# Layer-1 retention: transposes for identity matmuls, gate tiles moved around the scores, modulation steps paused

## The chip, the cores and the metric

One core of one Trainium2 chip runs the whole program. The engines are TensorE (PE: matmuls, with its weight loads shown as PEld), VectorE (DVE), ScalarE (ACT), GpSimd (POOL) and SyncE (SP, which here issues DMAs). The metric is device time in microseconds, the median of several runs. The profile is of one execution, with its own time.

## The reference, cut to what matters

The program is a two-layer backbone over 256 latent and 256 context tokens of width 1024. Each layer normalises and modulates the tokens, mixes them, adds the result, and then does the same with a SwiGLU feed-forward network (FFN). Layer 0 mixes by windowed attention and a gated linear recurrence, layer 1 by retention with 4 heads. The shift, scale and gate vectors of the modulation come from a product of the condition vectors with a 1024 x 6144 matrix for each layer.

For each retention head the reference computes, from the normalised streams h (1024 wide):

```
q, k (256 wide), v, g (512 wide)  = h @ w_in         # q and g for latent tokens only
q, k                              = rope(q), rope(k)  # latent tokens
o   = (decay * (q k^T)) v                             # both directions; keys: latent and context
y   = rms_norm(o) * silu(g)
out = concat over heads (y) @ w_out
```

## The kernel before, in words

Tokens lie along the free dimension, features on the 128 partitions. Every matmul operand is split into a high and a low part in float32r (hi = the rounded copy, lo = the rest), and a product is three matmuls: hi x hi, hi x lo, lo x hi (`mm3`, lines 333 to 338). Weights come as blocks of 128x128, 8 blocks to a piece: one DMA of 512 KB, a copy on ACT (line 268) and a subtraction on DVE (line 269). `take` hands out blocks in the order of the calls and splits two pieces ahead (`LOOK`); four split pieces exist at a time, so a fifth waits until the first has been used. A column tile of 128 outputs over the 8 blocks of the streams is one piece and 24 matmuls of 256 columns.

The text of the program is not the order of execution. A planner (the scheduler of the tile framework) sorts the instructions of each engine at compile time: the earlier an instruction is called, the higher its rank, but an instruction of lower rank goes first if the planner reckons that the engine would otherwise be idle. On the chip each engine then runs its list in order. So a wait appears where the planner's reckoning of another engine was too fast.

Small work is spread between the matmuls by ticks. `mm3` counts columns, and each 1600 columns call `tick`, which makes one step of each lane that is open and counts towards a modulation step: when the count reaches `modt`, one step is called and `modt` is taken off the count. A count goes on growing while `modt` is 10 ** 9. A modulation step loads 512 KB and makes one or two products of 128x1024 on DVE (line 233).

The retention runs head by head (lines 1171 to 1180). For each head: `ret_kq` makes K and Q, applies rope on DVE (`rope`, lines 1033 to 1039) and splits them; `ret_gate` makes two column tiles of the gate and applies Silu on ACT; `ret_scores` makes K^T Q, 24 matmuls from line 1106, multiplies by the decay matrix on DVE (line 1109) and splits; a second `ret_gate` makes the other two gate tiles; `ret_values` sums the token-major streams by the scores (`sums`) and projects the sums by the value weights (`project`); `ret_norm` (lane r) normalises and gates.

The token-major streams `htok` are made once, in head 0, by `tok_lane` (lane t, lines 1045 to 1057): for each of 4 token blocks and each half of the features, 4 pairs of matmuls against a float32r identity (`identr`) transpose hi and lo and add them in PSUM, and a split follows. `start` runs the lane's first step within `ret_kq(0)`, ahead of the rope; `drain` calls what is left of it before the values.

In head 0, K and Q come from `first_group`, which multiplies while the norm of the tokens is still being computed and corrects the result on DVE (`fix`); its four pieces are held until the context part of K is done.

Of the kernel before, what the change touches and what calls it, by code (L numbers as in the profile page):

```python
# [7 lines left out]
F32 = mybir.dt.float32  # L8
BF16 = mybir.dt.bfloat16
F32R = mybir.dt.float32r  # L10
I32 = mybir.dt.int32
AF = mybir.ActivationFunctionType
ALU = mybir.AluOpType
# [3 lines left out]
P = 128  # L17
D = 1024
KD = 8
L = 256  # L20
NT = 512
LAT = slice(0, 256)
# [10 lines left out]
N_PIECE = N_BLOCKS // PIECE  # L33
LOOK = 2
LN = 2
MODT = [4.6, 5.5, 4, 4]
QD = 3
FA = 2
PES = [3]
# [29 lines left out]
def hybrid_kernel(ctx, tc, xT, wst, mw0, mwT, small, cbc, cst, imask, dmat, out, order):  # L69
    nc = tc.nc  # L70
    V, A, T, G = nc.vector, nc.scalar, nc.tensor, nc.gpsimd

    cp = ctx.enter_context(tc.tile_pool(name="cp", bufs=1))
# [11 lines left out]
    def nm(s):  # L85
        uid[0] += 1
        return f"{s}_{uid[0]}"

    def u(shape=(P, NT), dt=F32):
        return up.tile(list(shape), dt, tag="u", name=nm("u"))  # L90
# [4 lines left out]
    def mmb():  # L95
        return pm.tile([P, NT], F32, tag="mm", name=nm("mm"))
# [37 lines left out]
    ident = con[:, C_ID:C_ID + P]  # L134
# [108 lines left out]
    modt = [MODE]  # L243
# [56 lines left out]
    def push(lane, gen):  # L300
        lanes.setdefault(lane, []).append(gen)
# [19 lines left out]
    def drain(lane):  # L321
        q = lanes.get(lane, [])
        while q:
            for _ in q.pop(0):
                pass
# [14 lines left out]
    def cut(a, s):  # L340
        return (a[0][:, s], a[1][:, s])
# [3 lines left out]
    def group(src, cols, ks, act, sls=(ALL,), kouter=True, banks=None):  # L345
        ps = banks or [mmb() for _ in cols]
        n = len(ks)
        ws = {}

        def one(i, j, sl):  # L350
            if (i, j) not in ws:
                ws[i, j] = take(src, ks[i], cols[j])
            mm3(ps[j][:, sl], ws[i, j], cut(act[i], sl), i == 0, i == n - 1)

        if len(sls) > 1 and not kouter:
            for j in range(len(cols)):
                for i in range(n):
                    one(i, j, sls[0])
            for sl in sls[1:]:
                for j in range(len(cols)):  # L360
                    for i in range(n):
                        one(i, j, sl)
            return ps
        for p, sl in enumerate(sls):
            if p:
                drain('c')
            if kouter and p == 0:
                for i in range(n):
                    for j in range(len(cols)):
                        one(i, j, sl)  # L370
            else:
                for j in range(len(cols)):
                    for i in range(n):
                        one(i, j, sl)
        return ps
# [151 lines left out]
    HS = [(a[:], b[:]) for a, b in h]  # L527

    K8 = list(range(8))
# [72 lines left out]
    def start(lane, gen):  # L602
        next(gen)
        push(lane, gen)
# [300 lines left out]
    tokgroup('ein', E_I, HS, itok_done)  # L905
    modt[0] = MODT[0]

    for hd in range(4):
        c = E_H + 3 * hd
        pg = group('ein', [c, c + 1, c + 2], K8, HS, kouter=False)  # L910
# [7 lines left out]
    for hd in range(4):  # L918
        pg = group('ein', [E_G + hd], K8, HS, kouter=False)
# [57 lines left out]
    def ffn(l, hs, streams, nxt, nl):  # L977
# [3 lines left out]
        for half in range(2):  # L981
            us = []
            jt = 0
            while jt < 11:
# [26 lines left out]
                jt += n  # L1011
                modt[0] = MODT[1 + 2 * l]
            if half == 1:
# [12 lines left out]
    ffn(0, hs, (0, 1), n1, nl)  # L1026
    HS = [(a[:], b[:]) for a, b in hh]

    modt[0] = MODT[2]
    O_K, O_Q, O_V, O_G = 0, 2, 4, 8  # L1030
    y1 = [None] * 16

# [5 lines left out]
            V.tensor_tensor(t[:, 1], d, rsin, ALU.mult)  # L1038
            V.tensor_tensor(o, t[:, 0], t[:, 1], op)

    identr = cp.tile([P, P], F32R, tag="idr", name="idr")
    A.activation(identr[:], ident, AF.Copy)
    htok = [[None, None] for _ in range(4)]

    def tok_lane():

        for st in range(4):
            for half in range(2):
                ps = axb((P, 4, P))
                for i in range(4):  # L1050
                    hi, lo = cut(HS[half * 4 + i], slice(st * P, (st + 1) * P))
                    T.matmul(ps[:, i, :], hi, identr[:], start=True, stop=False)
                    T.matmul(ps[:, i, :], lo, identr[:], start=False, stop=True)
                th, tl = u((P, 4, P), F32R), u((P, 4, P), F32R)
                split(ps[:], th[:], tl[:])
                htok[st][half] = (th, tl)
                yield
# [27 lines left out]
        split(qf[:], qhi[:], qlo[:])  # L1085
        return kk, (qhi, qlo)

    def ret_gate(hd, d2):
        c = 12 * hd + O_G + 2 * d2
        pg = group('oin', [c, c + 1], K8, HS, sls=(LAT,), kouter=False)  # L1090
        g = u((P, 2, L))
        for i in range(2):
            A.activation(g[:, i, :], pg[i][:, LAT], AF.Silu)
        return g

    def ret_scores(hd, kk, qq):
        dm = [u((P, 2, L)), u((P, 2, L))]
# [17 lines left out]
    def ret_values(hd, pp):  # L1115

        o = [mmb(), mmb()]
        gs = []

        def sums(k):  # L1120
            ps = axb()[:, 0:L]
            for st in range(4):
                mm3(ps, [t[:, k % 4, :] for t in htok[st][k // 4]], pp[st], st == 0, st == 3)
            t = u((P, 2, L), F32R)
            split(ps, t[:, 0], t[:, 1])
            gs.append((t[:, 0], t[:, 1]))

        def project(k):
            for dv in range(4):
                w = take('oin', k, 12 * hd + O_V + dv)  # L1130
                mm3(o[dv // 2][:, (dv % 2) * L:(dv % 2 + 1) * L], w, gs[k], k == 0 and dv % 2 == 0, k == KD - 1, True)

        sums(0)
        for k in range(1, KD):
            sums(k)
            project(k - 1)
        project(KD - 1)
        of, sqs = [], []
        for d2 in range(2):
            t, sq = u((P, 2, L)), u((P, 2, L))  # L1140
            tf = t[:].rearrange("p a b -> p (a b)")
            A.activation(tf, o[d2][:], AF.Copy)
            ra = A.activation(sq[:], t[:], AF.Square)
            of.append(t)
            sqs.append(sq)
        return of, sqs, ra

    def ret_norm(hd, of, sqs, ra, g):
        V.tensor_tensor(sqs[0][:], sqs[0][:], sqs[1][:], ALU.add)
        V.tensor_tensor(sqs[0][:, 0, :], sqs[0][:, 0, :], sqs[0][:, 1, :], ALU.add)  # L1150
        yield
        ss = axb()[:, 0:L]
        T.matmul(ss, ones, sqs[0][:, 0, :], start=True, stop=True)
        r = u()[:, 0:L]
        ln(r, ss, after=ra, exp=True, bias=epst[:], scale=1.0 / 512)
        A.activation(r, r, AF.Exp, scale=-0.5)
        for d2 in range(2):
            V.tensor_tensor(g[d2][:], g[d2][:], r.unsqueeze(1).to_broadcast([P, 2, L]), ALU.mult)
            V.tensor_tensor(of[d2][:], of[d2][:], g[d2][:], ALU.mult)
            yf[hd][d2] = of[d2]  # L1160
# [9 lines left out]

    for hd in range(4):
        kk, qq = ret_kq(hd)
        g = [ret_gate(hd, 0)]
        pp = ret_scores(hd, kk, qq)
        drain('r')
        if hd == 3:
            y_split(0)
        g.append(ret_gate(hd, 1))
        drain('t')
        o = ret_values(hd, pp)  # L1180
        start('r', ret_norm(hd, *o, g))
    for hd in range(1, 3):
        y_split(hd)
    drain('r')
# [134 lines left out]
```

## Time and profile before

| | us |
|---|---|
| median of 3 runs | 1146.19 (1146.14 to 1147.27) |
| the profiled execution | 1146.45 |
| its span in the trace | 1144.6 |
| PE busy | 1116.4 |
| PEld busy | 996.9 |
| DVE busy | 767.4 |
| ACT busy | 554.0 |
| POOL busy | 20.8 |

Times in rows are microseconds from the start of the span, if not marked ns. Matmuls overlap in the pipeline of PE, so the cost of one in a row of them is the distance between two starts, not its duration. In rows of the timeline and of the groups, what stands in brackets or behind the last bar is the time in which the engine was idle before, and what ended it. The DMA issues of SP and the DMA time are not shown here; the page has the hardware queue of SP at 47.6% of 16 engines' span.

### The profile page before, as it was taken

How to read it: one execution, taken by the hardware profiler on the slowest of the kernel's cores; microseconds unless marked ns; L12 is line 12 of the kernel's file. 1: busy time of each engine (PE TensorE's matmuls, PEld its weight loads, DVE VectorE, ACT ScalarE, POOL GpSimd, SP SyncE). 2: the span in 40 equal slices, each digit the busy share in tenths (PEclk: the TensorE clock that was granted, in tenths of full speed). 3: DMA queues.
4: the chain of work that ended last, by engine and by line, in shares of the span. 5: the costliest groups of instructions: out<-in, count | busy, mean ns of one | idle time of the engine just before them, and what ended most of it. 6: DMA issues, size and time to landing. Idle time of an engine off the chain costs nothing.

```text
span 1144.6 us, 18866 instructions
## 1 busy us (share of the span) xinstructions
PE 1116.4 (98%) x7514; PEld 996.9 (87%) x7514; DVE 767.4 (67%) x1399; ACT 554.0 (48%) x948; POOL 20.8 (2%) x46
## 2 busy tenths in 40 slices
PE   3999999999999999999999998999999999999998
PEld 1777877888998888988888898999999999999998
DVE  3877698899798557357883678374646577555553
ACT  5676676664753231123322476454445657544441
POOL 0012000000000000000000000000000000000000
PEclk9999999999999999999999999999999999999999
DMA  9987221326237446247983324343434265655553
GB/s 329 349 235 184 92 65 66 112 74 202 94 113 241 143 147 202 77 139 237 324 308 109 95 75 129 111 131 109 148 94 147 92 203 167 192 183 181 184 183 109
DMA packets 56121, 182.46 MB, mean 159 GB/s; under 512 B 6368, under 2 KB 9824, under 8 KB 55904
## 3 DMA queue, kind: packets, MB, share of 16 engines
q1 hardware_dynamic: 53648, 176.45, 47.6%
q0 software_dynamic: 2240, 4.72, 1.7%
q8 instruction: 59, 0.97, 0.4%
q14 instruction: 30, 0.25, 0.1%
q10 hardware_dynamic: 144, 0.08, 0.0%
HBM read 177.56 MB, written 1.05 MB: 156 GB/s over the span
## 4 chain that ended last, share of the span: by engine, by line
PE 84%; DVE 10%; ACT 3%; DMA 1%; issue 1%; DVEq 0%; ACTq 0%; SPq 0%
PE mm L338 23%; PE mm L337 23%; PE mm L336 23%; PE ax L337 2%; PE ax L336 2%; PE ax L338 2%; DVE wlo L269 2%; DMA raw<-in_wst_dram 1%; PE ax L175 1%; PE ax L656 1%; ACT whi L268 1%; PE ax L675 1%; DVE u L459 1%; PE mm L411 1%; PE mm L409 1%
## 5 line engine op out<-in xcount | busy, mean ns | idle before, releaser
L268 ACT ACTIVATE whi<-raw 128x1024 fp32r<-128x1024 f32 x230 | 243.3, 1059 | 403.0 <-PE mm L337 242.9
L269 DVE TENSOR_TENSOR wlo<-raw,whi 128x1024 fp32r<-128x1024 f32 x230 | 280.7, 1222 | 166.5 <-ACT whi L268 165.9
L336 PE MATMUL mm<-hh,whi 128*128 128x256 f32 (+1 forms) x1072 | 362.2, 339 | 1.2 <-ACT whi L268 0.9
L338 PE MATMUL mm<-hh,wlo 128*128 128x256 f32 (+1 forms) x1072 | 361.6, 338 | 0.6 <-DVE wlo L269 0.6
L337 PE MATMUL mm<-hl,whi 128*128 128x256 f32 (+1 forms) x1072 | 362.0, 338 | 0.1
L337 PE MATMUL mm<-u,whi 128*128 128x256 f32 (+2 forms) x768 | 236.9, 309 | 0.0
L338 PE MATMUL mm<-u,wlo 128*128 128x256 f32 (+2 forms) x768 | 236.7, 308 | 0.0
L336 PE MATMUL mm<-u,whi 128*128 128x256 f32 (+2 forms) x768 | 236.3, 308 | 0.3 <-DVE x L483 0.3
L338 PEld LDWEIGHTS mm<-hh,wlo 128*128 128x128 f32 x1072 | 204.4, 191 | 21.8 <-DVE wlo L269 0.8
L336 PEld LDWEIGHTS mm<-hh,whi 128*128 128x128 f32 x1072 | 204.2, 191 | 21.9 <-ACT whi L268 0.9
L337 PEld LDWEIGHTS mm<-hl,whi 128*128 128x128 f32 x1072 | 204.3, 191 | 20.2 <-DVE hl L466 0.3
L336 PEld LDWEIGHTS mm<-u,whi 128*128 128x128 f32 x768 | 146.4, 191 | 7.9 <-issue 0.4
L338 PEld LDWEIGHTS mm<-u,wlo 128*128 128x128 f32 x768 | 146.6, 191 | 7.2
L337 PEld LDWEIGHTS mm<-u,whi 128*128 128x128 f32 x768 | 146.6, 191 | 7.1
L233 DVE CUSTOM_DVE_ANT_0 mr<-mr,cb 128x1024 f32<-128x1024 f32 x72 | 87.1, 1222 | 13.2 <-DMA mr<-in_mwT_dram 12.6
L416 ACT ACTIVATE u<-u 128x512 fp32r<-128x512 f32 (+1 forms) x84 | 43.0, 526 | 36.7 <-DVE u L1007 17.3
L1007 DVE TENSOR_TENSOR u<-u,mm 128x512 f32<-128x512 f32 (+1 forms) x40 | 22.1, 553 | 44.7 <-PE mm L338 44.7
L233 DVE CUSTOM_DVE_ANT_0 u<-mr,cb 128x1024 bf16<-128x1024 f32 x40 | 48.4, 1219 | 2.8 <-DMA mr<-in_mwT_dram 1.5
L417 DVE TENSOR_TENSOR u<-u,u 128x512 fp32r<-128x512 f32 (+1 forms) x84 | 46.5, 565 | 5.0 <-ACT u L416 4.9
L336 PE MATMUL ax<-u,u 128*128 128x256 f32 x160 | 45.9, 287 | 3.1 <-ACT u L416 3.1
L483 DVE SCALAR_TENSOR_TENSOR x<-mm,modv,x 128x256 f32<-128x256 f32 x48 | 22.4, 480 | 36.1 <-PE mm L338 36.1
L337 PE MATMUL ax<-u,u 128*128 128x256 f32 x160 | 46.0, 287 | 0.0
(220 smaller groups left out, 1216.4 us busy)
## 6 DMA issues: line engine op xcount, KB each, us to landing
raw<-in_wst_dram SPq DMA_DIRECT2D x230, 512.0 KB, 3.8
mr<-in_mwT_dram SPq DMA_DIRECT2D x80, 512.0 KB, 4.5
u<-in_mw_dram SPq DMA_DIRECT2D x16, 256.0 KB, 5.2
u<-u POOLq DMA_DIRECT2D x20, 128.0 KB, 5.7
u<-in_dmat_dram POOLq DMA_DIRECT2D x8, 256.0 KB, 3.0
raw<-in_mw_dram SPq DMA_DIRECT2D x6, 256.0 KB, 5.2
mr<-in_mw_dram SPq DMA_DIRECT2D x6, 256.0 KB, 5.2
x<-in_xT_dram SPq DMA_DIRECT2D x8, 128.0 KB, 3.4
```

The costliest lines, as they stand in the source:

```text
L175: T.matmul(ps[32 * g:32 * g + 32, :], cT[:, k, :], mws[nt * 8 + k], start=(k < 4), stop=(k >= 4), skip_group_check=True)
L233: V.tensor_tensor_reduce(o, mr[:], cb[:, s, :], 1.0, 0.0, ALU.mult, ALU.add, mvec(l, s, ch, k))
L268: A.activation(hi[:], src[:], AF.Copy)
L269: V.tensor_tensor(lo[:], src[:], hi[:].bitcast(F32), ALU.subtract)
L336: T.matmul(o, w[0], a[0], start=first, stop=False, skip_group_check=shared)
L337: T.matmul(o, w[0], a[1], start=False, stop=False, skip_group_check=shared)
L338: anchor[0] = T.matmul(o, w[1], a[0], start=False, stop=last, skip_group_check=shared)
L409: T.matmul(ps[t][:], a[0], w[0], start=(k == 0), stop=False)
L416: A.activation(hi, src, AF.Copy)
L417: V.tensor_tensor(lo, src, hi.bitcast(F32), ALU.subtract)
L483: V.scalar_tensor_tensor(xs(m, s), ps[:, sl], mvec(l, s, ch, m), xs(m, s), ALU.mult, ALU.add)
L1007: V.tensor_tensor(g[:, 0:w], g[:, 0:w], ps[2 * i + 1][:, 0:w], ALU.mult)
```

## The change

`tok_lane` now adds hi and lo of a stream on DVE into a float32 tile (8 additions of 128x512 in all) and transposes that tile on PE against the plain identity, with the two halves of the features as the outer loop; `identr` is gone. The lane has 12 steps and an end in place of 8 and an end. `ret_gate` takes any gate tiles of a head: head 0 makes all four of its own tiles before its scores, every head but the last makes tiles 0 and 1 of the next head behind its scores, heads 1 and 2 make their tiles 2 and 3 before their scores, and head 3 makes tile 2 before and tile 3 behind. No modulation step is called in head 0 until the lane is drained; then the pace is 3.2 ticks a step instead of 4. The order of the weight blocks in memory follows the calls.

```diff
@@ -33,7 +33,7 @@
 N_PIECE = N_BLOCKS // PIECE
 LOOK = 2
 LN = 2
-MODT = [4.6, 5.5, 4, 4]
+MODT = [4.6, 5.5, 3.2, 4]
 QD = 3
 FA = 2
 PES = [3]
@@ -1026,7 +1026,7 @@
     ffn(0, hs, (0, 1), n1, nl)
     HS = [(a[:], b[:]) for a, b in hh]
 
-    modt[0] = MODT[2]
+    modt[0] = 10 ** 9
     O_K, O_Q, O_V, O_G = 0, 2, 4, 8
     y1 = [None] * 16
 
@@ -1038,19 +1038,22 @@
             V.tensor_tensor(t[:, 1], d, rsin, ALU.mult)
             V.tensor_tensor(o, t[:, 0], t[:, 1], op)
 
-    identr = cp.tile([P, P], F32R, tag="idr", name="idr")
-    A.activation(identr[:], ident, AF.Copy)
     htok = [[None, None] for _ in range(4)]
 
     def tok_lane():
 
-        for st in range(4):
-            for half in range(2):
+        for half in range(2):
+            full = []
+            for i in range(4):
+                hi, lo = HS[half * 4 + i]
+                if i % 2 == 0:
+                    yield
+                full.append(u())
+                V.tensor_tensor(full[i][:], hi.bitcast(F32), lo.bitcast(F32), ALU.add)
+            for st in range(4):
                 ps = axb((P, 4, P))
                 for i in range(4):
-                    hi, lo = cut(HS[half * 4 + i], slice(st * P, (st + 1) * P))
-                    T.matmul(ps[:, i, :], hi, identr[:], start=True, stop=False)
-                    T.matmul(ps[:, i, :], lo, identr[:], start=False, stop=True)
+                    T.transpose(ps[:, i, :], full[i][:, st * P:(st + 1) * P], ident)
                 th, tl = u((P, 4, P), F32R), u((P, 4, P), F32R)
                 split(ps[:], th[:], tl[:])
                 htok[st][half] = (th, tl)
@@ -1085,13 +1088,15 @@
         split(qf[:], qhi[:], qlo[:])
         return kk, (qhi, qlo)
 
-    def ret_gate(hd, d2):
-        c = 12 * hd + O_G + 2 * d2
-        pg = group('oin', [c, c + 1], K8, HS, sls=(LAT,), kouter=False)
-        g = u((P, 2, L))
-        for i in range(2):
-            A.activation(g[:, i, :], pg[i][:, LAT], AF.Silu)
-        return g
+    gates = [[None, None] for _ in range(4)]
+
+    def ret_gate(hd, *tiles):
+        c = 12 * hd + O_G
+        pg = group('oin', [c + i for i in tiles], K8, HS, sls=(LAT,), kouter=False)
+        for i, ps in zip(tiles, pg):
+            if i % 2 == 0:
+                gates[hd][i // 2] = u((P, 2, L))
+            A.activation(gates[hd][i // 2][:, i % 2, :], ps[:, LAT], AF.Silu)
 
     def ret_scores(hd, kk, qq):
         dm = [u((P, 2, L)), u((P, 2, L))]
@@ -1170,15 +1175,21 @@
 
     for hd in range(4):
         kk, qq = ret_kq(hd)
-        g = [ret_gate(hd, 0)]
+        if hd == 0:
+            ret_gate(0, 0, 1)
+        ret_gate(hd, *((2, 3) if hd < 3 else (2,)))
         pp = ret_scores(hd, kk, qq)
         drain('r')
         if hd == 3:
             y_split(0)
-        g.append(ret_gate(hd, 1))
+            ret_gate(3, 3)
+        else:
+            ret_gate(hd + 1, 0, 1)
         drain('t')
+        if hd == 0:
+            modt[0] = MODT[2]
         o = ret_values(hd, pp)
-        start('r', ret_norm(hd, *o, g))
+        start('r', ret_norm(hd, *o, gates[hd]))
     for hd in range(1, 3):
         y_split(hd)
     drain('r')
```

## Rows read from the trace of the kernel before

**Rows 1.** The page, part 1: engines, busy us (share of the span) x instructions
```profile
PE 1116.4 (98%) x7514; PEld 996.9 (87%) x7514; DVE 767.4 (67%) x1399; ACT 554.0 (48%) x948; POOL 20.8 (2%) x46
```
**Rows 2.** Waits of PE: who waited for whom: us in total, times, longest
```profile
PE ax L336 <- ACT u L416: 3.1, 1, 3.1
```
**Rows 3.** Stretches: length, busy us of PE, PEld, DVE, ACT, POOL, clock, DMA, GB/s
```profile
100.00:205.00 105.00, 104.36 (x827) 84.66 (x829) 85.07 (x233) 74.88 (x182) 3.18 (x8) 1.00 0.32 97
...
687.40:697.40 10.00, 9.99 (x84) 9.62 (x82) 9.81 (x21) 7.19 (x13) 0.00 (x0) 1.00 0.67 210
697.40:700.60 3.20, 0.06 (x2) 0.02 (x1) 2.47 (x6) 0.70 (x2) 0.00 (x0) 0.96 0.32 87
700.60:703.90 3.30, 3.30 (x16) 3.30 (x17) 3.04 (x5) 3.28 (x5) 0.00 (x0) 0.52 0.35 97
...
737.00:792.00 55.00, 54.95 (x412) 52.51 (x411) 29.66 (x45) 25.99 (x40) 1.09 (x2) 1.00 0.40 125
```
**Rows 4.** Timeline, all engines, head 0, end of Q: start, us, engine, line, operation
```profile
699.44 0.42 DVE L1039 TENSOR_TENSOR u<-u 128x256 f32<-128x256 f32 x1
699.90 0.63 ACT L416 ACTIVATE u<-u 128x512 fp32r<-128x512 f32 x1 [3.08 <-DVE u L1039]
...
700.56 0.69 DVE L417 TENSOR_TENSOR u<-u,u 128x512 fp32r<-128x512 f32 x1 [0.70 <-ACT u L416]
...
700.58 0.58 PE L336 MATMUL ax<-u,u 128*128 128x256 f32 x1 [3.14 <-ACT u L416]
```
**Rows 5.** Groups by line, PE, 685.8 to 714: count | busy us, mean ns | idle before
```profile
L1053 PE MATMUL ax<-idr,hl 128*128 128x128 f32 x32 | 7.6, 277 | 0.0
```
**Rows 6.** Timeline of PE around the first group of `tok_lane`
```profile
687.30 0.28 PE L338 MATMUL ax<-hh,wlo 128*128 128x256 f32 x1
687.42 0.22 PE L1052 MATMUL ax<-idr,hh 128*128 128x128 f32 x1
...
688.44 0.28 PE L337 MATMUL mm<-hl,whi 128*128 128x256 f32 x1
```
**Rows 7.** Timeline of PE around four transposes in layer 0's attention
```profile
114.46 0.60 PE L656 MATMUL ax<-con,u 128*128 128x128 f32 x4
...
115.13 0.39 PE L627 MATMUL ax<-u,u 128*128 128x512 f32 x1
115.35 0.39 PE L336 MATMUL mm<-hh,whi 128*128 128x512 f32 x1
```
**Rows 8.** Groups by line, DVE, 685.8 to 714
```profile
L417 DVE TENSOR_TENSOR u<-u,u 128x512 fp32r<-128x512 f32 x5 | 3.4, 690 | 1.6 <-ACT u L416 1.6
```
**Rows 9.** Timeline of DVE, head 0: splits of `tok_lane`
```profile
691.19 0.68 DVE L417 TENSOR_TENSOR u<-ax,u 128x512 fp32r<-128x512 f32 x1
...
702.65 1.88 DVE L417 TENSOR_TENSOR u<-ax,u 128x512 fp32r<-128x512 f32 x3
```
**Rows 10.** Timeline, all engines, head 3: Q, first score, last split of the scores
```profile
864.67 0.42 DVE L1037 TENSOR_TENSOR u<-mm,con 128x256 f32<-128x256 f32 x1
...
868.07 0.43 DVE L1039 TENSOR_TENSOR u<-u 128x256 f32<-128x256 f32 x1
...
868.56 0.61 ACT L416 ACTIVATE u<-u 128x512 fp32r<-128x512 f32 x1
...
868.69 1.23 DVE L269 TENSOR_TENSOR wlo<-raw,whi 128x1024 fp32r<-128x1024 f32 x1 [0.20 <-ACT whi L268]
...
869.83 0.69 DVE L417 TENSOR_TENSOR u<-u,u 128x512 fp32r<-128x512 f32 x1
870.40 0.28 PE L336 MATMUL ax<-u,u 128*128 128x256 f32 x1
...
875.91 0.69 DVE L417 TENSOR_TENSOR u<-u,u 128x512 fp32r<-128x512 f32 x1 [0.70 <-ACT u L416]
```
**Rows 11.** Line 233, the modulation products: duration ns min/median/max, first and last start
```profile
L233 DVE CUSTOM_DVE_ANT_0 mr<-mr,cb x72: 1211/1221/1227, 49.9 to 599.6; 128x1024 f32<-128x1024 f32 x72
L233 DVE CUSTOM_DVE_ANT_0 u<-mr,cb x40: 1196/1218/1226, 47.6 to 535.8; 128x1024 bf16<-128x1024 f32 x40
```

## The prediction, made before the result was known

> **What bounds the kernel now.** I read the page first: TensorE (PE) is busy 98% of the span [rows 1]. So a change pays only by taking work off PE or by closing one of its few waits. The waits of PE came next: in the code that the change touches there is one, 3.1 us, in which the first score matmul of a head waited for ScalarE (ACT) [rows 2]. The table by stretches places it. In head 0, from 697.4 to 700.6, PE does 0.06 us of work while VectorE (DVE) is busy 2.47 us; the next 3.3 us run at a granted clock of 0.52, that is at the 1.2 GHz level; then it is 1.00 again. Head 1's stretch is full, 54.95 of 55 us (the stretches of heads 2 and 3 are alike; one row stands for them) [rows 3]. The retention therefore loses 3.14 us of waiting and 3.3 x 0.48 = 1.6 us of slow clock, 4.7 us together, and all of it in head 0. The timeline shows why: the last rope operation of Q ends at 699.86 on DVE, ACT writes the high half of Q from 699.90, DVE the low half from 700.56 to 701.25, and the score starts at 700.58 [rows 4]. DVE is the bound of that stretch, PE only waits for it.
>
> **Transposes for identity matmuls.** Before, each of 8 groups takes 8 matmuls against the identity, 32 of each of two lines (one row stands for both) [rows 5]. A group starts at 687.42; the second gate matmul behind it starts at 688.44; one gate matmul takes 0.12 (687.30 to 687.42) [rows 6]; so a group costs 1.02 - 0.12 = 0.90 us of PE, and eight cost 7.2. The new form, a 128x128 f32 transpose against the plain identity, stands in the attention of layer 0: four start at 114.46, the matmul after the next starts at 115.13, the one between takes 0.22 (115.13 to 115.35), so four cost 0.45 [rows 7], and eight groups 3.6. PE work saved: 3.6 us. This term is the surest, because nothing has to overlap for it to count.
>
> A weighed rule: the attention's transposes (line 656) lie between 100 and 205 us, and that stretch has a granted clock of 1.00 [rows 3], the 2.4 GHz level. The Trainium skill ("TensorE: Matmul & The Clock Gate", Part 4) says that transposes don't count as PE activity as matmuls do and that the full clock does not engage for them. By that rule the clock could fall around the new groups, and by the row it doesn't; here they come four at a time between matmuls, as there.
>
> The price is on DVE: eight additions of 128x512 f32. The nearest row is the same sort of operation on two such tiles, 690 ns [rows 8]; three splits of that size in a row took 1.88 [rows 9], so one more takes 0.60. Eight take 4.8 us. The 8 splits behind the transposes stay. Removing the copy of the identity saves one small ACT operation long before; I put it at nothing, both ways.
>
> **Gate tiles around the scores.** All 16 tiles remain, each 8 blocks x 3 matmuls x 0.12 = 2.88 us of PE; only their places change. Head 0 gets four ahead of its scores instead of two, then two of head 1. In heads 1 and 2 the two ahead and two behind remain in form. Head 3 has one ahead and one behind.
>
> *Head 0.* From 687.42, PE has 96 gate matmuls = 11.5 us, so it reaches the scores at 698.9, or later by 0.45 for each transpose group that is ready. Q was complete at 701.25. In its favour: the first group's split, which stood ahead of the rope at 691.19 [rows 9], now comes after it (-0.6). Against it: additions that are put in where DVE waits for ACT, none to two (+0 to 1.2). So Q is complete at 700.6 to 701.9, and PE waits 1.7 to 3.0, less up to three groups (1.35). I take 1.6, and expect no fall of the clock at that: the one fall in these rows followed a wait of 3.1. Bounds: 0; and if all eight additions stand ahead of Q, it is 4.2 late (4.8 - 0.6), PE waits about 4.1 and pays 1.5 of slow clock, 5.6.
>
> After the scores start, PE has 24 score matmuls (2.9), two gate tiles (5.8) and the transposes (3.6), 12.3 us to the first value sums at about 712.8. DVE by then owes three weight splits of 1.2 (3.6), about seven additions (4.2), the decay products and splits of the scores (4 x 0.6) and the first half's splits (4 x 0.6): 12.6 us from 701.2, so 713.8. I take a second wait of 1.0; bounds 0, and 3.2 if the second half's four splits (2.4) also come first. They need not: the sums use the first half alone until the fifth.
>
> *Head 3.* Q's rope starts at 864.67, when Q's matmuls end, and ends at 868.50; ACT has the high half at 869.17, DVE the low half at 870.52, and the score starts at 870.40 [rows 10]. That fits two tiles exactly. With one tile, PE arrives at 870.40 - 2.88 = 867.5 and the high half is there 1.6 to 1.7 later, the low half earlier than before only if the weight split at 868.69 steps aside. Putting the other tile first doesn't help: scores would then end where they did, with nothing left to cover their split, whose last part DVE finished at 876.6 [rows 10], 3.0 us after the 24 score matmuls (24 x 0.12 behind 870.40, and 0.28 for the last to end). I take a loss of 1.8. Bounds: 0 (both weight splits of 1.2 step aside), and 4.7, which is what head 0's wait and its slow clock cost.
>
> **The modulation steps.** The pause and the new pace act on steps that are called during the retention. But the trace has the last modulation product at 599.6, all 72 + 40 of them done [rows 11], 100 us ahead of the wait in head 0: the planner puts these steps into DVE's free time far ahead of where the program calls them. They wait for nothing of the retention, so their place in the program should not matter. I cost this edit at nothing; the free DVE time of the FFN hides it.
>
> **Sum.** 3.6 (PE work) + 4.7 (old wait and slow clock) - 1.6 - 1.0 (new waits in head 0) - 1.8 (head 3) = 3.9 us less. The profiled execution took 1146.45 (span 1144.6 and 1.85 around it), 0.26 over the median of 1146.19; on the median: 1142.3.
>
> **Rivals.**
> *Full cover.* Q is no later than PE, and the planner keeps the weight splits out of the chains. Then waits of some 0.6 remain: 8.3 - 0.6 = 7.7 less, 1138.5. For it: the transposes fill PE exactly while it would wait. Against it: DVE is busy 9.81 of 10 us before the wait [rows 3] and gets 4.8 more.
> *Additions ahead of Q.* Head 0 waits 4.1 and the clock falls again (5.6 in all); the values then wait no further, since the additions are done. 8.3 - 5.6 - 1.8 = 0.9 less, 1145.3. For it: half an addition's room opens wherever DVE waits for ACT. Against it: the old splits of the lane's later groups, ready before 697, were placed behind Q, at 702.65 [rows 9]. The rule of the Trainium skill on transposes, if it held, would end near here too: one fall of the clock, 1.6 us.
> *Modulation comes into the retention (slower).* If the planner no longer reaches the later calls, the steps saved up in the pause go out one a tick after head 0. By the columns that the code counts, I estimate that 27 of the 80 steps are called in the retention (at 5.5 ticks a step the FFN's calls end near step 53). A step's product is 1.22 us of DVE [rows 11]. Head 1's Q and score chains have no slack (as head 3's rows show [rows 10]), and two steps ahead of each cost 2.4 + 2.4, with a fall of the clock 1.6: 6.4 more than the forecast, 1148.7. It decides once more than three steps stand in such chains (3.7 us; the forecast's gain is 3.9). Against it: not one of the 112 products ran after 600 us, though many were called later.
>
> **How the numbers follow.** What a measurement of this kernel can tell from no change is about 0.2%, 2.3 us: faster means below 1143.9, slower above 1148.5. Forecast 0.50, with its own range 1140.0 to 1144.3, of which 0.43 is faster and 0.07 the same; full cover 0.17, faster; additions ahead of Q 0.22, of which 0.20 the same and 0.02 faster; modulation or a like loss 0.11, slower. Faster 0.62, same 0.27, slower 0.11. The range runs from full cover with all bounds at zero (1138.0) to past the additions' case with head 3 at 3.5 us instead of 1.8 (1147.0).
>
> **What would show it.** Right: 32 transposes in place of 64 identity matmuls, groups of four costing 0.45; in head 0 a wait before the scores of 1 to 2 us and no stretch at 0.5 of the clock; a new wait of 1 to 2.5 us before head 3's scores or values; heads 1 and 2 as long as before; no modulation product after 601 us. Wrong: a wait of over 3 us in head 0 with a slow stretch behind it; head 3 without a wait or with more than 3 us; modulation products between 690 and 800 us; or a difference that lies outside the retention.

## The result: slower, and the profile after

| | before | after |
|---|---|---|
| median, us (runs beside each other) | 1146.73 (1146.14 to 1147.48) | 1156.83 (1155.62 to 1158.53) |
| the profiled execution, us | 1146.45 | 1155.62 |
| its span, us | 1144.6 | 1153.8 |

The ratio is 1.0089, with a 95% interval from 1.0071 to 1.0106. The forecast of 1142.3 us missed the sign.

First the engines on the page of after, against [rows 1]: PE is busy 3.3 us longer, although it runs fewer matmuls. Then the waits of PE, against [rows 2].

```profile
PE 1119.7 (97%) x7482; PEld 997.3 (86%) x7482; DVE 771.3 (67%) x1407; ACT 554.1 (48%) x947; POOL 20.9 (2%) x46
```

```profile
PE ax L1056 <- DVE u L1052: 8.8, 3, 6.2
...
PE ax L336 <- DVE u L417: 0.8, 1, 0.8
```

Before, PE waited once in this code, 3.1 us for Q. Now its transposes (line 1056) wait 8.8 us for DVE's additions (line 1052). The stretches of head 0 show where, against [rows 3]: length, busy us of PE, PEld, DVE, ACT, POOL, granted clock, DMA share, GB/s.

```profile
687.00:700.00 13.00, 13.00 (x109) 12.86 (x108) 12.13 (x23) 9.72 (x16) 0.00 (x0) 1.00 0.65 198
700.00:706.30 6.30, 0.12 (x2) 0.06 (x2) 5.60 (x11) 2.15 (x3) 0.00 (x0) 0.79 0.79 218
706.30:709.00 2.70, 2.70 (x12) 2.23 (x13) 1.69 (x3) 0.37 (x1) 0.00 (x0) 0.50 0.26 103
...
719.00:722.00 3.00, 1.59 (x10) 0.82 (x8) 3.00 (x6) 1.69 (x2) 0.00 (x0) 1.00 0.55 175
722.00:726.00 4.00, 1.87 (x9) 1.29 (x10) 2.95 (x6) 1.71 (x5) 0.00 (x0) 0.77 0.38 131
726.00:730.00 4.00, 4.00 (x20) 4.00 (x20) 1.92 (x4) 1.30 (x3) 0.00 (x0) 0.50 0.02 4
...
688.39:751.12 62.73, 53.02 (x394) 50.59 (x393) 37.15 (x61) 27.70 (x47) 1.10 (x2) 0.89 0.37 112
```

PE does its 96 gate matmuls without a gap, then stands still for 6.2 us, works at the 1.2 GHz level, and has a second group of gaps from 719 to 726, again with half the clock behind it. The last row is the whole of head 0, from its first gate matmul to head 1's first. The same stretch of the kernel before, from the end of the context part to the end of the values:

```profile
687.42:737.10 49.68, 46.53 (x379) 46.12 (x378) 30.26 (x51) 24.80 (x43) 1.09 (x2) 0.97 0.40 121
```

Two gate tiles more lie in head 0 now, 48 x 0.12 = 5.76 us; so 49.68 compares as 55.44, and PE busy 46.53 as 52.29. Head 0 is 7.3 us longer: 6.6 us of idle PE (62.73 - 53.02 = 9.71 against 3.15), and 0.7 us of busy PE, although some 3.6 us of work went. Slow clock took most of these 4.3: summed over the trace, busy time times the missing part of the clock is 5.15 us, against 1.59 before. Head 3 is 1.1 us longer (from the last value matmul of head 2 to its own: 55.20, against 59.90 - 5.76). The other 1.0 us of the 9.2 us of span was there before head 0: the context part ended at 688.27 instead of 687.30. Up to there the order of the work is the same, and in the other kernels with that order (all but adds_pool) it ended between 686.45 and 688.10, so I take this part for scatter between executions. The profiled execution of after is also the fastest of its four: the medians lie 10.1 us apart, and the last microsecond of that is in no trace. Heads 1 and 2 are as long as before (55.0 us each).

Why PE waits is in the timeline of DVE and ACT in after, against [rows 4] and [rows 9]: start, duration, engine, line, operation, idle time before.

```profile
697.99 1.23 DVE L269 TENSOR_TENSOR wlo<-raw,whi 128x1024 fp32r<-128x1024 f32 x1 [0.87 <-ACT whi L268]
...
700.50 1.22 DVE L269 TENSOR_TENSOR wlo<-raw,whi 128x1024 fp32r<-128x1024 f32 x1
...
702.64 1.22 DVE L269 TENSOR_TENSOR wlo<-raw,whi 128x1024 fp32r<-128x1024 f32 x1
...
704.23 0.63 ACT L416 ACTIVATE u<-u 128x512 fp32r<-128x512 f32 x1 [2.06 <-DVE u L1039]
...
704.89 0.69 DVE L417 TENSOR_TENSOR u<-u,u 128x512 fp32r<-128x512 f32 x1 [0.69 <-ACT u L416]
705.50 2.49 DVE L1052 TENSOR_TENSOR u<-hh,hl 128x512 f32<-128x512 f32 x4
```

On PE, the sixteen transposes in one row, and the first score:

```profile
706.24 3.85 PE L1056 MATMUL ax<-con,u 128*128 128x128 f32 x16 [6.17 <-DVE u L1052]
710.01 0.58 PE L336 MATMUL ax<-u,u 128*128 128x256 f32 x1
```

Three things are to be seen. Three weight splits more than before stand ahead of Q on DVE. Line 440 corrects K and Q in two pairs of operations; behind the first pair there are eight splits where there were five (behind the second pair, six where there were three). The first four additions stand behind Q's split. And on PE the sixteen transposes that need those additions stand ahead of the scores. So PE waits for Q and then for the additions too. Most of the wait is Q: its high half was there at 704.86, and PE had been through with its gate tiles at 700.07.

### The profile page after: what moved, and what is told of

Same layout as the page of the kernel before. It is cut to its first block, busy times and chain, and to the rows that moved or that the text cites. A ratio compares the mean times of both kernels' runs of the same rounds, so it can differ in the third digit from the quotient of the medians.

```text
span 1153.8 us, 18813 instructions
## 1 busy us (share of the span) xinstructions
PE 1119.7 (97%) x7482; PEld 997.3 (86%) x7482; DVE 771.3 (67%) x1407; ACT 554.1 (48%) x947; POOL 20.9 (2%) x46
## 4 chain that ended last, share of the span: by engine, by line
PE 90%; DVE 7%; ACT 2%; issue 1%; DMA 1%; DVEq 0%; ACTq 0%
PE mm L338 24%; PE mm L336 24%; PE mm L337 24%; PE ax L337 3%; PE ax L336 3%; PE ax L338 3%; DVE wlo L269 2%; PE ax L175 1%; PE ax L656 1%; PE ax L675 1%; PE mm L411 1%; PE mm L409 1%; PE mm L410 1%; DVE u L744 1%; PE ax L453 0%
## 5 line engine op out<-in xcount | busy, mean ns | idle before, releaser
L268 ACT ACTIVATE whi<-raw 128x1024 fp32r<-128x1024 f32 x230 | 243.3, 1059 | 406.2 <-PE mm L337 241.0
L417 DVE TENSOR_TENSOR u<-ax,u 128x256 fp32r<-128x256 f32 (+1 forms) x44 | 21.4, 493 | 39.2 <-ACT u L416 39.1
```

The costliest lines, as they stand in the source:

```text
L268: A.activation(hi[:], src[:], AF.Copy)
L417: V.tensor_tensor(lo, src, hi.bitcast(F32), ALU.subtract)
```

## The experiments

All follow head 0 and are told by one table. Length is from the end of the context part to the end of head 0's values, with 5.76 us added where two gate tiles fewer lie in it; idle is PE's idle time in that stretch; Q is how long after the last correction (line 440 in the kernels with the original line numbers) the low half of Q starts on DVE, with the number of weight splits ahead of it behind the first two of the four corrections. Where the text compares kernels in us, it compares their medians, unless it says head 0.

| kernel | length | idle | Q, splits | median us | ratio to before, 95% interval |
|---|---|---|---|---|---|
| before | 55.4 | 3.15 | 10.8, 5 | 1146.7 to 1147.3 | |
| after | 62.7 | 9.71 | 14.2, 8 | 1156.83 | 1.0089 [1.0071, 1.0106] |
| gates_only | 54.1 | 1.78 | 10.8, 5 | 1146.86 | 0.9998 [0.9990, 1.0007] |
| tok_only | 62.3 | 10.71 | 14.5, 8 | 1153.00 | 1.0054 [1.0041, 1.0068] |
| pause_only | 55.4 | 3.14 | 10.8, 5 | 1147.23 | 1.0003 [0.9994, 1.0013] |
| adds_pool | 58.5 | 8.92 | 15.3, 8 | 1154.76 | 1.0070 [1.0056, 1.0084] |
| no_adds | 52.4 | 3.83 | 13.5, 8 | 1145.36 | 0.9987 [0.9977, 0.9996] |
| adds_early | 56.8 | 8.31 | 16.7, 8 | 1149.91 | 1.0022 [1.0013, 1.0031] |
| gates_spread | 51.5 | 0.50 | 10.9, 5 | 1144.39 | 0.9974 [0.9964, 0.9983] |
| half_tr | 49.7 | 0.49 | 10.8, 5 | 1142.04 | 0.9960 [0.9947, 0.9972] |
| fewer_splits | 61.4 | 8.92 | 12.7, 5 | 1153.74 | 1.0056 [1.0042, 1.0070] |
| late_half_only | 54.6 | 3.38 | 10.8, 5 | 1145.67 | 0.9985 [0.9976, 0.9994] |
| splits_behind | 58.6 | 6.25 | 10.0, 5 | 1150.51 | 1.0032 [1.0021, 1.0042] |
| no_adds_behind | 52.0 | 4.62 | 10.1, 5 | 1144.85 | 0.9985 [0.9976, 0.9994] |

### The three parts of the change alone

**gates_only**: `ret_gate` and the loop over the heads as changed, `tok_lane` and the pace as before.

```diff
-        g = [ret_gate(hd, 0)]
+        if hd == 0:
+            ret_gate(0, 0, 1)
+        ret_gate(hd, *((2, 3) if hd < 3 else (2,)))
```

> The gate tiles moved as in the changed kernel, with the old tok_lane (identity matmuls) and no pause. Theory A (the changed kernel loses because its transposes hang on additions that stand behind Q on DVE, and without the identity matmuls between the gate tiles PE uses up weight pieces sooner, so three more weight splits come into Q's chain): here nothing waits for DVE between the gates; 96 gate matmuls and 7 groups of 0.90 us cover 687.4 to 705, Q is complete near 701 with 5 weight splits ahead as before, so no wait and no slow clock in head 0, 5 us gained, head 3 loses 0.8: 1142 us. Rival B (moving the gate tiles is what costs, since four tiles need four weight splits ahead of Q and head 3 has too little cover): slower than before, 1149 or more, with a wait of 3 us or more ahead of head 0's scores.

Measured 1146.86: no loss, and not the gain that theory A gave it. Q's wait went, as expected, but another came. PE's waits and two stretches:

```profile
PE ax L1052 <- DVE u L417: 1.8, 1, 1.8
```

```profile
703.00:706.00 3.00, 1.81 (x13) 1.84 (x14) 2.24 (x4) 2.97 (x7) 0.00 (x0) 0.89 0.47 157
706.00:709.00 3.00, 3.00 (x18) 3.00 (x16) 2.52 (x3) 1.95 (x5) 0.00 (x0) 0.54 0.05 18
```

```profile
703.36 1.88 DVE L417 TENSOR_TENSOR u<-ax,u 128x512 fp32r<-128x512 f32 x3
...
704.19 0.30 PE L1052 MATMUL ax<-idr,hh 128*128 128x128 f32 x1 [1.78 <-DVE u L417]
```

An identity group, the sixth, can't start, because the four PSUM buffers `ax` are held by earlier groups whose splits stand behind Q on DVE; it starts when the first of the three splits in the row has ended. So the gate tiles are not the harm, and the work that PE does while it waits for Q (its fill) must not hang on DVE in any way, buffers included.

**tok_only**: the new `tok_lane`, all else as before.

```diff
-                    T.matmul(ps[:, i, :], hi, identr[:], start=True, stop=False)
-                    T.matmul(ps[:, i, :], lo, identr[:], start=False, stop=True)
+                    T.transpose(ps[:, i, :], full[i][:, st * P:(st + 1) * P], ident)
```

> The new tok_lane alone (additions on DVE, transposes), gate tiles and modulation as before the change. Theory A: PE waits about 6 us for the first additions, which stand behind Q on DVE, the clock falls to about 0.5 behind that wait, and more waits follow ahead of the values: 1150 to 1153 us. Rival B (the gate tiles cost): the 3.6 us of PE work are gained and the old wait stays: about 1143.

```profile
PE ax L1056 <- DVE u L1052: 10.7, 2, 6.4
```

As theory A has it: the loss of head 0 is here (62.3 against 62.7 in after), with the same eight splits ahead of Q and a wait of 6.4 us where after has 6.2. But the three parts alone don't add up to the change: 1153.00 is 3.8 us less than after. Head 3, which this kernel leaves as it was, is 1.1 of that; 1.8 is the earlier end of the context part in the profiled execution (686.45 against 688.27). The rest is not explained.

**pause_only**: the pause and the new pace, all else as before.

```diff
-MODT = [4.6, 5.5, 4, 4]
+MODT = [4.6, 5.5, 3.2, 4]
...
-    modt[0] = MODT[2]
+    modt[0] = 10 ** 9
...
+        if hd == 0:
+            modt[0] = MODT[2]
```

> The pause of the modulation steps and the pace of 3.2 alone. Both theories A and B: no difference, 1146 to 1147 us, last modulation product near 600 us. Rival C (the pause moves modulation work or DMAs in the plan): 1149 or more, products later than 601 us.

Measured: the same time, and on every engine the same list of instructions as before.

### Is it the additions?

**adds_pool**: the changed kernel, additions on POOL.

```diff
-                V.tensor_tensor(full[i][:], hi.bitcast(F32), lo.bitcast(F32), ALU.add)
+                G.tensor_tensor(full[i][:], hi.bitcast(F32), lo.bitcast(F32), ALU.add)
```

> The changed kernel with the eight additions on POOL in place of DVE. Theory A: the additions are done before PE has the first transpose (no wait there); Q's chain still holds 8 weight splits, so the scores wait about 3 us for Q and the clock falls once; no waits ahead of the values: 1145 to 1149 us. Rival D (the transposes themselves cost the clock or the time, wherever the additions are done, or POOL and DVE hinder each other): within 2 us of the changed kernel, 1154 to 1158, with slow clock around each group of transposes.

The transposes no longer wait, but Q is still later (15.3) and PE waits 6.3 us for it. And PE waits ahead of head 0, 3.0 us in all, for DVE's normalised streams (line 466); its context part ends at 691.15, about 3 us or more behind the other kernels, which the length of head 0 in the table leaves out:

```profile
PE ax L337 <- DVE hl L466: 2.0, 2, 1.2
PE mm L337 <- DVE hl L466: 1.0, 1, 1.0
```

DVE beside POOL's additions, both timelines:

```profile
678.36 4.23 POOL L1052 TENSOR_TENSOR u<-hh,hl 128x512 f32<-128x512 f32 x3 [444.50 <-DVE hl L466]
...
688.00 7.04 POOL L1052 TENSOR_TENSOR u<-hh,hl 128x512 f32<-128x512 f32 x3 [2.12 <-DVE hl L466]
```

```profile
688.17 0.47 DVE L466 SCALAR_TENSOR_TENSOR hl<-u,modv,hh 128x256 fp32r<-128x256 f32 x1
...
689.83 0.41 DVE L440 TENSOR_TENSOR u<-mm,u 128x256 f32<-128x256 f32 x1
690.16 3.76 DVE L269 TENSOR_TENSOR wlo<-raw,whi 128x1024 fp32r<-128x1024 f32 x2
693.84 1.49 DVE L466 SCALAR_TENSOR_TENSOR hl<-u,modv,hh 128x256 fp32r<-128x256 f32 x1
```

Two weight splits take 3.76 us here, 2.34 in after (from 687.51), and line 466 takes 1.49 instead of 0.47. The rival in which POOL and DVE hinder each other fits.

**no_adds**: the high parts are transposed directly.

```diff
-                full.append(u())
-                V.tensor_tensor(full[i][:], hi.bitcast(F32), lo.bitcast(F32), ALU.add)
+                full.append(hi.bitcast(F32))
```

> The changed kernel with the additions left out: the high parts are transposed as they are, so the low parts of the value streams are left out of the result; everything else stays. Theory A (the wait before the transposes is the wait for DVE's additions, and DVE's three more weight splits ahead of Q, 3.4 us, are a second loss that stays): the transposes go between the gate tiles, PE waits for Q by some 2.5 us instead of 6.2 for the additions, and the waits before the values (3.4 us) go: 1146 to 1150. Rival E (the additions are all of the loss): Q comes as in the kernel before, 1140 to 1143. Rival T (the transposes themselves, or a clock that falls around them): 1153 to 1157, with stretches at half clock that follow no wait.

```profile
PE ax L336 <- DVE u L417: 3.8, 1, 3.8
```

11.5 us less than after, just below theory A's range and above rival E's. Against before the whole loss is gone (0.9987), but only half of the 3.9 us that were forecast is gained (1.9): Q still comes late behind eight splits, and PE waits 3.8 us. Q was complete at 704.7; the last 0.7 us go to the first split behind it (704.66 to 705.3), which frees an `ax` buffer as in gates_only. The transposes themselves are cleared. A group of four stands here between gate matmuls at full clock:

```profile
690.90 0.28 PE L338 MATMUL mm<-hh,wlo 128*128 128x256 f32 x1
691.02 0.60 PE L1055 MATMUL ax<-con,hh 128*128 128x128 f32 x4
691.38 0.36 PE L336 MATMUL mm<-hh,whi 128*128 128x256 f32 x1
```

It costs 691.38 - 691.02 = 0.36 us, a little less than the 0.45 of the prediction.

**adds_early**: the first half's additions called ahead of the rope.

```diff
-                if i % 2 == 0:
+                if half and i % 2 == 0:
                     yield
...
+            if not half:
+                yield
             for st in range(4):
```

> The changed kernel with the first half's four additions called ahead of the rope, so that they rank ahead of Q; nothing is left out. Theory A (DVE's work up to Q is the bound, whatever its order): the transposes go between the gate tiles and no longer wait, but Q is complete 2.4 us later than in the changed kernel, and the wait moves to the scores: 5 to 6 us there, then a stretch at half clock; 1152 to 1156. Rival O (only the order is wrong: transposes ranked ahead of the scores that hang on additions ranked behind Q): the wait shrinks to about 2 us, 1146 to 1149.

Measured 1149.91, between the two ranges. The transposes don't wait, Q is 2.5 us later than in after, and PE waits 7.0 us for it: that is theory A. But the second group of waits shrank to one of 1.3 us with no slow stretch behind it (724 to 730: 1.00). Theory A had charged the order with nothing; it is worth some 7 us of the 10 (5.9 of them in head 0). What the parts are worth does not add up to 10: where two waits overlap, taking away one leaves the other.

### Is it the weight splits ahead of Q?

**fewer_splits**: in after, the last three weight splits ahead of Q are left out.

```diff
-            r = q
+            r, skip = q, q in (109, 110, 111)
...
+            lo = pieces[q - 1][1] if skip else wp.tile([P, PIECE, P], F32R, tag="wlo", name=nm("wlo"))
...
+            None if skip else V.tensor_tensor(lo[:], src[:], hi[:].bitcast(F32), ALU.subtract)
```

> The changed kernel without the three weight splits that stand last ahead of Q on DVE (the three pieces use the low part of the piece before, so those gate tiles come out wrong); the order of all else stays. Theory A (everything ahead of the additions on DVE's list is paid by the transposes behind them on PE's): Q and the additions come 3.4 us earlier, the first wait shrinks from 6.2 to 2.8 us, the waits before the values stay; 1152 to 1154. Rival W (the weight splits sit in time in which DVE would wait for ACT anyway): the wait stays at 5 us or more, 1155 to 1157.

The time is in theory A's range, but the mechanism is not as it had it: Q came 1.5 us earlier, not 3.4, and the wait was 4.7. Head 0 is 1.3 us shorter than in after; the rest of the difference between the medians lies outside it, so that the time fell into the range is luck. DVE and ACT show what else held Q:

```profile
701.19 1.06 ACT L268 ACTIVATE whi<-raw 128x1024 fp32r<-128x1024 f32 x1 [1.10 <-DMA raw<-in_wst_dram]
702.15 0.61 ACT L416 ACTIVATE u<-u 128x512 fp32r<-128x512 f32 x1
...
702.80 0.69 DVE L417 TENSOR_TENSOR u<-u,u 128x512 fp32r<-128x512 f32 x1 [1.79 <-ACT u L416]
```

The rope was done at 701.0. But ACT, in its list, had a copy of a weight piece ahead of Q's, and that copy waited for its DMA.

**splits_behind**: in after, the copies and splits of these three pieces are ordered behind Q's; nothing is left out.

```diff
+            if q in (109, 110, 111):
+                with tc.issue_after(behind[0].ins):
+                    A.activation(hi[:], src[:], AF.Copy)
+                with tc.issue_after(behind[1].ins):
+                    V.tensor_tensor(lo[:], src[:], hi[:].bitcast(F32), ALU.subtract)
```

> The changed kernel, in which three weight pieces (those of the gate tiles behind the scores) are copied on ACT and split on DVE behind Q's own copy and split; nothing is left out. Theory A2 (ahead of Q stood not only DVE's three splits, 3.4 us, but ACT's three copies, each of which waits for its DMA; without the splits alone the wait shrank by 1.5 us only): Q's low half starts 10.8 to 11 us behind the last correction of the first group on DVE, as in the kernel before, instead of 14.2; the first wait of PE is 2.8 to 3.2 us instead of 6.2; the waits before the values stay; 1152 to 1154. Rival L (the pieces are then late for the gate tiles behind the scores, and PE waits there): Q as early, but 1155 or more.

```profile
PE ax L1063 <- DVE u L1059: 4.5, 3, 1.9
```

```profile
700.13 0.69 DVE L1095 TENSOR_TENSOR u<-u,u 128x512 fp32r<-128x512 f32 x1 [0.69 <-ACT u L1095]
```

(Line 1063 is after's 1056, 1059 its 1052; the row is the low half of Q.) Q came 4.2 us earlier than in after, the longest wait fell from 6.2 to 1.9, the pieces were late for nobody, and the time fell by more than theory A2 said: the ratio is 1.0032 instead of 1.0089. So of the ten microseconds some six, by the medians, are three weight pieces that the planner put ahead of Q; in the profiled executions it is 4.6 of the 9.2, 4.1 of it in head 0.

**no_adds_behind**: both at once, no additions and these pieces behind Q.

```diff
-                V.tensor_tensor(full[i][:], hi.bitcast(F32), lo.bitcast(F32), ALU.add)
...
+                with tc.issue_after(behind[1].ins):
```

> The changed kernel without the additions (the high parts are transposed as they are, the low parts of the value streams are left out) and with those three weight pieces behind Q. Theory A2 (the additions and the weight pieces ahead of Q are all of the loss): PE reaches the scores some 14 us behind the context's last matmul and Q is there; no wait over 1 us and no stretch at half clock in head 0; 1139.5 to 1142. Rival F (without the identity matmuls PE is short of fill in any order): a wait of 2 us or more before the scores or the value sums; 1143 to 1146.

Here theory A2 failed and rival F held: 1144.85, hardly better than no_adds. PE's waits, and DVE around the first of them:

```profile
PE ax L343 <- DVE u L424: 4.6, 2, 2.7
```

```profile
700.08 0.69 DVE L1094 TENSOR_TENSOR u<-u,u 128x512 fp32r<-128x512 f32 x1 [0.70 <-ACT u L1094]
701.03 1.23 DVE L273 TENSOR_TENSOR wlo<-raw,whi 128x1024 fp32r<-128x1024 f32 x1 [0.26 <-PE mm L344]
702.17 0.68 DVE L424 TENSOR_TENSOR u<-ax,u 128x512 fp32r<-128x512 f32 x1
...
703.00 0.35 PE L343 MATMUL ax<-u,u 128*128 128x256 f32 x1 [1.88 <-DVE u L424]
```

Q was complete at 700.8, PE was through with its gate tiles at 701.1, and still the score started at 703.0: at the end of the first split of a transposed group, which frees an `ax` buffer. That is the wait of gates_only, at the scores. PE runs out of fill that hangs on nothing else.

### What pays instead

**gates_spread**: gate tiles as changed, identity matmuls as before, four groups (first half) ahead of the scores and four within head 0's values, whose first four sums need the first half alone.

```diff
         for k in range(1, KD):
             sums(k)
             project(k - 1)
+            if hd == 0 and k < 3:
+                tok_group(2 * k - 2, 1)
+                tok_group(2 * k - 1, 1)
```

> The gate tiles moved as in the change, no pause, identity matmuls as before; the four groups of the first half are called ahead of the scores, the four of the second half within head 0's values, which need them only from the fifth sum on. Theory A (fill that waits for nothing DVE owes covers Q): 96 gate matmuls and four groups, 15.1 us, cover Q's chain; no wait over 1 us in head 0 and no stretch at half clock there; against the kernel before 4.7 us less in head 0 and 0.8 more in head 3: 1142 to 1144. Rival B (a wait comes back elsewhere, as with the gate tiles moved alone, for instance before the value sums): 1146 to 1148.

**half_tr**: the same, with additions and transposes for the second half.

```diff
+            if hd == 0 and k == 1:
+                full = []
+                for hi, lo in HS[4:]:
+                    full.append(u())
+                    V.tensor_tensor(full[-1][:], hi.bitcast(F32), lo.bitcast(F32), ALU.add)
+            if hd == 0 and k in (2, 3):
+                tok_group2(full, 2 * k - 4)
+                tok_group2(full, 2 * k - 3)
```

> The same, but the second half in the values is made by additions and transposes in place of identity matmuls. Theory A (additions and transposes pay where DVE has room and PE doesn't): 1.8 us of PE less than with identity matmuls, 1140 to 1142.5. Rival B (additions in the values hold up the sums' splits, so PE waits there): 1143 to 1147, with waits of PE for DVE between the first and the fifth sum.

As theory A, though gates_spread is 0.4 us above its range: head 0 is 4.0 us shorter than before, and head 3 takes 1.1 of it back. Head 0 of gates_spread and of half_tr:

```profile
688.22:739.67 51.45, 50.95 (x426) 50.50 (x425) 32.60 (x53) 27.36 (x47) 1.10 (x2) 1.00 0.44 138
```

```profile
687.79:737.51 49.72, 49.23 (x411) 48.70 (x409) 34.76 (x57) 27.15 (x47) 1.10 (x2) 1.00 0.46 142
```

PE is idle for 0.5 us and the clock stays at 1.00. half_tr is 1.7 us shorter in head 0, where 1.8 were expected of the transposes, and it beats both kernels: 0.9960 [0.9947, 0.9972] to before.

**late_half_only**: half_tr's streams with the gate tiles as before (against half_tr; the other calls of `ret_gate` go back too).

```diff
-        if hd == 0:
-            ret_gate(0, 0, 1)
-        ret_gate(hd, *((2, 3) if hd < 3 else (2,)))
+        g = [ret_gate(hd, 0)]
...
```

> The gate tiles as in the kernel before; the first half by identity matmuls ahead of the scores, the second by additions and transposes in head 0's values. Theory A (the gate tiles and the late half work only together): the wait of 3.1 us before the scores and its stretch at half clock stay, and the 1.8 us of PE saved are lost to a wait before the value sums, which lost 3.6 us of fill; 1146 to 1148.5. Rival G (the late half alone is the gain; the gate tiles add nothing to it): 1142 to 1145.

```profile
PE ax L336 <- ACT u L416: 3.1, 1, 3.1
```

Measured 1145.67, just below theory A and above rival G. The old wait of 3.1 us stays, as A said, but the wait before the sums that was to eat the saving did not come; in head 0 0.9 us of the 1.8 is left. Neither part pays much alone (0.9998 and 0.9985), both together 0.9960: the gate tiles cover Q (keep PE busy until it is there) only if the groups don't need buffers before Q is split, and the groups can leave the cover only if gate tiles take their place.

## Why the prediction was wrong, step by step

**The bound was read rightly, but not in full.** That PE only waits in the stretch before the scores, and mostly for DVE, is what the experiments show. But DVE's busy time was not all of the limit: in fewer_splits Q waited for a copy in ACT's list and its DMA, and in gates_only and no_adds_behind PE waited for an `ax` buffer.

**PE work saved, 3.6 us: right in size, worth nothing in its place.** 32 transposes took the place of 64 identity matmuls, at 0.36 us a group between matmuls instead of the 0.45 predicted. But head 0 was the one stretch in which PE waited for DVE. "This term is the surest, because nothing has to overlap for it to count" is false there: in such a stretch PE's own work is cover (time in which it does not wait), and less cover is a longer wait. It paid only where PE was full (half_tr, in the values).

**"So Q is complete at 700.6 to 701.9": the step that failed.** PE came to the scores when the prediction had it (700.07, with head 0 starting 1.0 later in this execution), but the low half of Q ended at 705.6: behind the last correction it came 3.4 us later than before (14.2 against 10.8). I counted additions that might slip ahead of Q; what slipped ahead were three weight pieces. In the kernels here, Q has five weight splits ahead of it wherever identity groups called ahead of the rope stand between the first gate tiles, and eight where they don't, apart from the three kernels in which I took the pieces away. That PE's faster pace through its weight pieces in the planner's reckoning is what invites them is argued from these lists; only their price is shown, by splits_behind: 4.2 us of Q and 0.6% of the time. That price includes ACT's copies and their DMAs, which the prediction did not look at.

**"Less up to three groups (1.35). I take 1.6": failed too.** I took the transposes as fill that is ready while PE waits for Q. They hang on additions that stand behind Q, yet stand ahead of the scores on PE. A wait that was to be 1.6 was 6.2, and it ended with the first addition (started at 705.50), not with Q. The bound that I gave for this (all eight additions ahead of Q, 5.6 with the clock) was the wrong direction: the first four cost more behind Q than ahead of it, as adds_early shows (1149.91 against 1156.83).

**"I take a second wait of 1.0", bound 3.2: the bound was about right.** Three waits of 0.8, 1.8 and 0.8 us stand ahead of the value sums, 3.4 together, and a second slow stretch that was not in the sum. In all, slow clock took some 3.6 us more in head 0 than before (5.15 against 1.59).

**Head 3, 1.8: an overestimate.** It lost 1.1 us. With its single tile before the scores PE had no wait over 0.3 us there, since the planner put seven gate matmuls behind the first two score matmuls.

**The modulation steps, nothing: right.** The last product ran at 601.2, against 599.6 in [rows 11]; that is 0.2 past the limit of 601 named in the prediction, but 87 us ahead of head 0:

```profile
L233 DVE CUSTOM_DVE_ANT_0 mr<-mr,cb x72: 1212/1220/1227, 50.5 to 601.2; 128x1024 f32<-128x1024 f32 x72
```

and pause_only alone changed no list. So the slower rival had the right sign by a mechanism that did not occur.

**The rule on transposes and the clock** (the Trainium skill, "TensorE: Matmul & The Clock Gate", Part 4) is not what slowed the kernel. The slow stretches of before and of gates_only, which have no transposes in head 0, follow waits as those of after do. And in half_tr two runs of eight transposes stand among matmuls with the clock at 1.00:

```profile
719.70:724.40 4.70, 4.70 (x44) 4.70 (x43) 2.75 (x4) 2.66 (x5) 0.00 (x0) 1.00 0.24 56
```

## What to carry to other kernels

Where an engine waits for another, its own work is cover: before you make it cheaper, ask what will stand in its place, and whether that hangs on the engine that is late, through data, through its queue or through a buffer. A cheaper form that moves work to the busier engine belongs in a stretch where that engine has room (here the values, not the scores). And an edit that lets one engine run ahead lets prefetch run ahead too: look at what the planner then puts ahead of the critical operation on every engine, ACT's copies that wait for a DMA among them.

## What the runs showed of the hardware that was not expected

POOL and DVE delay each other, and not evenly. In the rows of adds_pool three POOL additions took 7.04 us that had taken 4.23 ten microseconds earlier; in those 7 us line 466 took 0.47 at its first run and 1.49 at the next shown, and two weight splits 3.76. The Trainium skill ("SBUF — State Buffer", section "SBUF: two separate sides") says that DVE and GpSimd share a pair of ports that one instruction holds until it ends (on DVE's side one with two SBUF inputs, among others), while the other waits. The rows agree. Taken singly, the three additions end at 690.59, 692.83 and 695.04, and between them the two weight splits end at 691.68 and 693.91 and line 466 at 695.33: from 690.2 on the two engines take turns, and each operation ends no more than its usual duration (1.3 for an addition, 1.2 for a split, 0.47 for line 466) after the other engine's.

The length of one wait does not say whether the clock falls behind it: 1.8 us in gates_only was followed by 0.54, while in no_adds_behind waits of 1.9 and 2.7 us were followed by 1.00:

```profile
703.00:706.00 3.00, 2.93 (x23) 2.76 (x23) 2.72 (x3) 2.97 (x5) 0.00 (x0) 1.00 0.81 198
...
718.00:721.00 3.00, 3.00 (x27) 3.00 (x26) 1.15 (x3) 0.77 (x2) 0.00 (x0) 1.00 0.07 26
```

What decides between them no run here settles.
